# The gate and up products of two feed-forward networks, in a fixed order of slots of one block product

## The chip, the core and the metric

The kernel runs on one core of a Trainium2 chip. It uses five engines, each with a queue of its own that it works through in order: TensorE (PE, with PEld for its weight loads), VectorE (DVE), ScalarE (ACT), GpSimd (POOL), and SyncE (SP), which issues all the DMAs. The metric is the device time of one execution in microseconds; the median of three runs of the kernel before is 2160.37 us (2160.37 to 2164.31).

## The reference

One step of a streaming encoder layer for 1024 + 32 frames of width 1024. It holds two feed-forward networks, one before and one after the token mixer; the change touches these two alone.

```python
def swiglu(h, w_gate, w_up, w_down):
    return (jax.nn.silu(h @ w_gate) * (h @ w_up)) @ w_down

def layer(x, lw, sb_fn, s0, gla_chunk):
    x = x + 0.5 * swiglu(rmsnorm(x, g_ffn1), w1g, w1u, w1d)
    mix, k, v, s = token_mixer(rmsnorm(x, g_mix), ...)
    x = x + mix
    x = x + 0.5 * swiglu(rmsnorm(x, g_ffn2), w2g, w2u, w2d)
    return rmsnorm(x, g_final), k, v, s
```

The inner width is 2816, that is 22 tiles of 128.

## The kernel before, in words

**Numbers in halves.** Every factor of a matmul is stored as a high and a low half: ACT copies the value with rounding into the high half (L94, in `split_to`), DVE subtracts that from the value and leaves the low half (L98). A block product is three matmuls per pair of tiles (high by high, high by low, low by high).

**Gate and up.** A pair of 128-wide tiles of the gate or of the up weights, by all 1056 columns, is one `Step`, computed by Strassen's scheme with seven block products instead of eight. There are 20 steps for each network, even ones for gate and odd ones for up; the first pair is done without Strassen by `Opening`. One block product (`product`, L378) is 24 matmuls of 264 columns. The seven come in the order 1, 6, 7, 5, 2, 4, 3 (`ORDER`); I number their places 0 to 6 and call the time of one product on PE a slot. The seven use four PSUM tiles, `acc_a` to `acc_d`, each of which is one of four buffers: a serves places 0 and 4, b place 1, c places 2 and 5, d places 3 and 6. `after` (L391 to L428) reads a PSUM tile out behind its product: on ACT at place 0 (`s1`, L391), on DVE as `u2` and `u3` at places 1 and 2 (L394, L397), then the four results (L418 or L427 on DVE with a Silu on ACT or a product on POOL; place 4 by ACT or DVE alone). A product that goes on with a PSUM tile waits until it has been read out.

**Beside the products** run three kinds of work:
- the weights of the next step: `load` brings them raw (L330, L331), POOL forms the sums S1 to S4 (L349 to L362), `split_to` makes halves of them (`S1` to `S4`, `A22`, and `whl` for the two unsummed blocks, L98);
- the operands of the down product that follows: `form` (L442) takes differences of finished tiles, `keep` makes halves and stores them (`part_spill`, L451);
- in the first network alone, chores (`Splits`): 52 pieces of the weights that the mixer uses later are loaded (`x<-win`, 256 KB, L77), halved, and stored (`win_split<-x`, 512 KB, L84). They share two buffers in turn, which are parts of the big tile `x`.

**What sets the order.** `gate_up` writes each product down and behind it, at once, all that the product allows: both halves of the next weights, both halves and the store of a finished operand, and a chore's load, halves or store (job n from slot 5n/2 on: load there, halves 3 slots on, store 4 on). The list scheduler of the framework then orders the instructions of each engine by its own estimate of when each is ready. So neither the distance between a first half and a second one, nor the pace of the chores, is fixed by the program: the 52 chores, written over 130 of the 140 slots, ran between 89 and 390 us.

**Down.** `DownStep.prep` forms four sums on POOL and their halves for one Strassen step of the down product; `Down.head` is called at the last gate-and-up step and loads the first operands (`load_part`, L620) and weights (`load_step`, L624). Loads of `x` (L515) into the four tiles that chores and kept operands used stand in `gate_up`'s last step.

Of the kernel before, what the change touches and what calls it, by code (L numbers as in the profile page):

```python
# [54 lines left out]
class Splits:  # L55
# [3 lines left out]
    def __init__(self, S, jobs, bufs):  # L59
        self.S, self.jobs, self.bufs = S, jobs, bufs  # L60
        self.at = {}
        for n in range(2 * len(jobs)):
            slot = 5 * n // 2
            for k, fn in ((0, self.load), (3, self.split), (4, self.store)):
                self.at.setdefault(slot + k, []).append((fn, n))

    def buf(self, n):
        return self.bufs[n % 2][:, :1024]

    def halves(self, n):  # L70
        return self.buf(n).rearrange("p (a n) -> p a n", a=2)

    def cols(self, n):
        return slice(n % 2 * 512, n % 2 * 512 + 512)

    def load(self, n):
        self.S.nc.sync.dma_start(self.buf(n)[:, 512:], self.jobs[n // 2][0][:, self.cols(n)])  # L77

    def split(self, n):
        t = self.halves(n).bitcast(F32R)  # L80
        split_to(self.S, t[:, 0], t[:, 1], self.buf(n)[:, 512:])

    def store(self, n):
        self.S.nc.sync.dma_start(self.jobs[n // 2][1][:, :, self.cols(n)], self.halves(n))  # L84

    def some(self, slot):
        for fn, n in sorted(self.at.pop(slot, ()), key=lambda job: job[1]):
            fn(n)
# [228 lines left out]
class Step:  # L317
# [15 lines left out]
    def split_w(self):  # L333
        w = self.S.wp.tile([P, 2, 1024], F32R, name="whl", tag="w")
        split_to(self.S, w[:, 0], w[:, 1], self.raw0)
        self.W["A11"], self.W["A12"] = w[:, :, :512], w[:, :, 512:]

    def prep(self, p, eng):
# [25 lines left out]
        split_to(S, w[:, 0], w[:, 1], src)  # L364
# [80 lines left out]
    def keep(self, name, src):  # L445

        S = self.S
        S.n_kept = getattr(S, "n_kept", 0) + 1
# [18 lines left out]
def gate_up(S, H, op, steps, among, between, tail, xd, chore):  # L467


    N = len(steps)  # L470
    done = {}

    def prep(t, p):
        if t >= N:
            return
        steps[t].prep(p, S.nc.gpsimd if t else S.nc.vector)
        done[t] = done.get(t, 0) + 1
        if done[t] == 5 and t + 2 < N:
            steps[t + 2].load()

    for j in range(4):
        for n, i in enumerate((0, 1, 2, 3) if j < 3 else (0, 2, 1, 3)):
            op.product(j, i, among(j, n))
            between(j, n)
            if i == 2:
                op.silu()
            if j == 3 and n == 1:
                steps[0].split_w()
                for p in (6, 7, 5):
                    prep(0, p)  # L490
        op.store(j)
        if j == 1:
            steps[0].load()
            steps[1].load()
    for k in range(4):
        H.part("T3", k, 1)
    for p in (4, 3):
        prep(0, p)
    for t in range(N):
        for p in ORDER:  # L500
            steps[t].product(p)
            steps[t].after(p)
            n = ORDER.index(p)
            for back, name in FORMS[t % 2].get(n, ()):
                if t >= back:
                    steps[t - back].form(name)
# [5 lines left out]
            if t == N - 1:  # L512
                if p == 1:
                    for d in range(4):
                        S.nc.sync.dma_start(S.x[d], xd[d])  # L515
                tail(p)
# [10 lines left out]
class DownStep:  # L527
# [6 lines left out]
    def prep(self, raw):  # L534
# [6 lines left out]
        s1, s2, s3, s4 = s12[:, :w], s12[:, w:], s34[:, :w], s34[:, w:]  # L541
        nc.gpsimd.tensor_add(s1, a[3], a[2])
        nc.gpsimd.tensor_sub(s2, s1, a[0])
        nc.gpsimd.tensor_sub(s3, a[0], a[3])
        nc.gpsimd.tensor_sub(s4, a[1], s2)
        tag = ("S1", "A22") if self.odd else ("S2", "S3")
# [5 lines left out]
        split_to(S, wb[:, 0, :w], wb[:, 1, :w], a[2])  # L552
# [43 lines left out]
class Down:  # L596
# [35 lines left out]
    def prep(self, i):  # L632
        if i < len(self.steps):
            self.steps[i].prep(self.raw.pop(i))

    def head(self, p):
# [7 lines left out]
        elif p == 7:  # L644
            self.load_part(0, 4)
            self.load_part(0, 5)
            self.prep(0)
        elif p == 5:
            self.load_part(0, 6)

# [792 lines left out]
def body(tc, A):  # L1443
# [10 lines left out]
    with ExitStack() as top:  # L1454
# [66 lines left out]
        with ExitStack() as es:  # L1521
# [41 lines left out]
            gate_up(S, H, op, steps, among, between, down.head, A["x"], splits.some)  # L1563
# [136 lines left out]
        with ExitStack() as es:  # L1700
# [68 lines left out]
            gate_up(S, H, op, steps, lambda j, n: [], between, down.head, xs, lambda n: None)  # L1769
# [112 lines left out]
```

## Time and profile before

| what | value |
|---|---|
| median of three runs | 2160.37 us |
| the profiled execution's own time | 2163.55 us |
| its span on the core | 2161.8 us |
| PE busy | 2067.5 us (96%) |
| DVE busy | 1454.9 us (67%) |
| ACT busy | 887.7 us (41%) |
| POOL busy | 668.8 us (31%) |
| data moved by DMA | 325.03 MB, 150 GB/s on average |

How to read it: PE is nearly always busy, so the time is PE's own work and the holes in it. An average over the span hides where the holes are; the page's row of PE by 40 slices of 54 us shows 7 tenths in the first slice, then 9, 9, 9, 9, 8, 8 (54 to 378 us), where 9 stands for anything from 90% up, and nines after that. A row of a table of windows gives, for each engine, its busy time and in brackets its number of instructions that began there, then the granted TensorE clock, the share of the DMA engines and what they moved. A row of the waits names who waited for whom, the sum, how often, and the longest wait.

### The profile page before, as it was taken

To read this page: it belongs to the slowest core of one execution; us is meant where nothing else is said; L and a number is where in the kernel's file an instruction comes from. 1 tells how busy PE (TensorE), PEld (TensorE's weight loads), DVE (VectorE), ACT (ScalarE), POOL (GpSimd) and SP (SyncE) were. 2 spreads that over 40 slices of the span, in tenths; PEclk is the share of its full clock that TensorE was granted. 3 is DMA by queue.
4 is the path that set the end of the run, shared out by engine and by line. 5 is a ranking of instruction groups with operands and counts; after the bars stand their busy time and mean duration, and the time that the engine had idled before them with its cause. 6 is when DMAs were issued, how large, how long until landed. Compare 5 with 4: busy or idle time off the path is not lost.

```text
span 2161.8 us, 38696 instructions
## 1 busy us (share of the span) xinstructions
PE 2067.5 (96%) x15636; PEld 1997.3 (92%) x15636; DVE 1454.9 (67%) x2205; ACT 887.7 (41%) x1618; POOL 668.8 (31%) x578
## 2 busy tenths in 40 slices
PE   7999988999999999999999998999999999999997
PEld 6898988999999988888889987899999999999997
DVE  6866677664778556376776677687566666457865
ACT  6543444432223333243654555454333433322333
POOL 0133333444775110011112201101343443458720
PEclk9999999999999999999999999999999999999999
DMA  4277777546854121112133243242334334398322
GB/s 173 81 254 259 262 267 269 204 161 249 339 193 125 69 77 59 63 63 85 37 101 98 78 135 106 85 134 80 120 141 156 142 130 160 129 379 299 108 65 81
DMA packets 128339, 325.03 MB, mean 150 GB/s; under 512 B 12096, under 2 KB 32864, under 8 KB 124832
## 3 DMA queue, kind: packets, MB, share of 16 engines
q1 hardware_dynamic: 128160, 322.56, 42.6%
q8 instruction: 123, 2.02, 0.4%
q14 instruction: 56, 0.46, 0.1%
HBM read 201.72 MB, written 114.03 MB: 146 GB/s over the span
## 4 chain that ended last, share of the span: by engine, by line
PE 69%; DVE 11%; DMA 7%; issue 6%; POOL 4%; ACT 3%; SPq 0%; DVEq 0%; ACTq 0%; POOLq 0%
PE acc_a L378 8%; PE acc_d L378 8%; PE acc_c L378 7%; PE acc L286 4%; PE pj L103 4%; PE acc_b L378 4%; PE pj L105 3%; PE pj L104 3%; PE pd_c L574 3%; PE pd_d L574 3%; PE pd_a L574 3%; PE pd L103 2%; PE pd L105 2%; PE pd L104 2%; DMA win_split<-x 2%
## 5 line engine op out<-in xcount | busy, mean ns | idle before, releaser
L378 PE MATMUL acc_a<-h,whl 128*128 128x264 f32 x1920 | 251.4, 287 | 11.5 <-ACT s L391 9.5
L378 PEld LDWEIGHTS acc_a<-h,whl 128*128 128x128 f32 x1920 | 242.3, 191 | 12.9 <-ACT s L391 10.8
L378 PE MATMUL acc_d<-part,S 128*128 128x264 f32 x1920 | 247.3, 284 | 3.7 <-DVE x L418 3.6
L378 PEld LDWEIGHTS acc_d<-part,S 128*128 128x128 f32 x1920 | 238.7, 188 | 4.7 <-DVE x L418 4.3
L94 ACT ACTIVATE x<-x 128x528 fp32r<-128x528 f32 (+1 forms) x164 | 103.4, 638 | 295.8 <-POOL x L428 81.5
L98 DVE TENSOR_TENSOR x<-x 128x528 fp32r<-128x528 f32 (+1 forms) x164 | 132.1, 814 | 132.7 <-ACT x L94 132.0
L103 PE MATMUL pj<-h,whl 128*128 128x352 f32 x576 | 205.3, 356 | 0.0
L105 PE MATMUL pj<-h,whl 128*128 128x352 f32 x576 | 190.9, 331 | 0.0
L104 PE MATMUL pj<-h,whl 128*128 128x352 f32 x576 | 189.3, 329 | 0.0
L94 ACT ACTIVATE S<-s 128x512 fp32r<-128x512 f32 x160 | 98.2, 623 | 114.7 <-PE acc_d L378 43.1
L428 POOL TENSOR_TENSOR x<-tc,x 128x528 f32<-128x528 f32 x60 | 103.3, 1722 | 123.4 <-DVE tc L427 110.7
L362 POOL TENSOR_TENSOR s<-wraw,s 128x512 f32<-128x512 f32 x38 | 49.8, 1312 | 295.2 <-DVE S L98 295.2
L378 PE MATMUL acc_c<-h,A 128*128 128x264 f32 x960 | 126.7, 288 | 10.1 <-DVE u L397 9.8
L378 PEld LDWEIGHTS acc_c<-h,A 128*128 128x128 f32 x960 | 121.8, 190 | 12.3 <-DVE u L397 12.3
L378 PE MATMUL acc_b<-h,S 128*128 128x264 f32 x960 | 124.7, 285 | 1.5 <-ACT h L94 1.1
L98 DVE TENSOR_TENSOR S<-s,S 128x512 fp32r<-128x512 f32 x160 | 120.8, 756 | 6.3 <-ACT S L94 5.6
L378 PE MATMUL acc_c<-part,S 128*128 128x264 f32 x960 | 123.8, 284 | 1.1 <-DVE hid L298 1.1
L378 PEld LDWEIGHTS acc_b<-h,S 128*128 128x128 f32 x960 | 120.5, 188 | 1.9 <-ACT h L94 1.3
L378 PEld LDWEIGHTS acc_c<-part,S 128*128 128x128 f32 x960 | 119.5, 188 | 1.3 <-DVE hid L298 1.3
L592 POOL TENSOR_TENSOR x<-x,u 128x528 f32<-128x528 f32 x64 | 102.9, 1615 | 49.7 <-DVE x L563 49.4
L103 PEld LDWEIGHTS pj<-h,whl 128*128 128x128 f32 x576 | 110.5, 192 | 5.1 <-issue 1.7
L349 POOL TENSOR_TENSOR s<-wraw 128x512 f32<-128x512 f32 x38 | 51.7, 1360 | 201.4 <-DVE S L98 195.2
(343 smaller groups left out, 4952.3 us busy)
## 6 DMA issues: line engine op xcount, KB each, us to landing
part_spill<-x SPq DMA_DIRECT2D x112, 528.0 KB, 2.8
h<-part_spill SPq DMA_DIRECT2D x64, 528.0 KB, 8.9
part<-part_spill SPq DMA_DIRECT2D x48, 528.0 KB, 9.6
win_split<-x SPq DMA_DIRECT2D x44, 512.0 KB, 4.0
whl<-win_split SPq DMA_DIRECT2D x22, 1024.0 KB, 5.0
wraw<-w1g SPq DMA_DIRECT2D x22, 512.0 KB, 4.8
wraw<-w1u SPq DMA_DIRECT2D x22, 512.0 KB, 4.0
x<-win SPq DMA_DIRECT2D x44, 256.0 KB, 3.6
```

Of the source, the lines that this page charges most:

```text
L94: nc.scalar.activation(hi, src, AF.Copy)
L98: nc.vector.tensor_sub(lo, src, hi.bitcast(F32))
L103: nc.tensor.matmul(out, w[:, 0, wsl], a[:, 0, asl], start=first, stop=False)
L104: nc.tensor.matmul(out, w[:, 0, wsl], a[:, 1, asl], start=False, stop=False)
L105: nc.tensor.matmul(out, w[:, 1, wsl], a[:, 0, asl], start=False, stop=last)
L286: nc.tensor.matmul(out, self.w[i](k, a), quarter(S, k, b, j), start=k == 0 and n == 0, stop=k == KT - 1 and n == 2)
L349: eng.tensor_add(self.s1, a21, a22)
L362: eng.tensor_sub(src, a12, self.s2)
L378: nc.tensor.matmul(t[:, s, :SW], w[:, a, ks], m(k, b, s), start=fresh and k == 0 and n == 0, stop=k == 3 and n == 2, skip_group_check=not ...
L428: nc.gpsimd.tensor_mul(two(hid), t, sg)
L574: nc.tensor.matmul(t[:, s, :SW], w[:, u, k * P : k * P + P], b[:, v, ss(s)], start=fresh and k == 0 and i == 0, stop=k == 1 and i == 2, sk ...
L592: nc.gpsimd.tensor_add(x[r][h], x[r][h], u)
```

## The change

- `Slots` keeps a list of work by slot. `later(k, fn)` puts `fn` k slots on; `split(hi, lo, src, k, then)` puts the high half k slots on, the low half k + 1, and what follows (a store) k + 2. `run` does what stands at the present slot.
- A step's sums are still formed at once on POOL; their high halves come one slot later and their low halves two later (`whl`: in the same slot and the next). A kept operand: high half one slot after it is formed, low half two, store three after.
- A chore that begins at slot k = 5n/2: load at k, high half at k + 2, low half at k + 3, store at k + 4.
- In each slot the read-out of the product stands ahead of the halves, and the halves ahead of the differences and sums.
- The 140 slots are recorded under a manual schedule for all five engines: each engine keeps the order in which the program is written.
- Weights are loaded for the step after next at place 1 of each step. The first down step's sums stay at place 2 (`p == 7`) and its halves move to place 4 (`p == 2`).

```diff
+class Slots:
+    def __init__(self, S):
+        self.S, self.now, self.at = S, 0, {}
+    def later(self, k, fn):
+        self.at.setdefault(self.now + k, []).append(fn)
+    def split(self, hi, lo, src, k, then=None):
+        nc = self.S.nc
+        self.later(k, lambda: nc.scalar.activation(hi, src, AF.Copy))
+        self.later(k + 1, lambda: nc.vector.tensor_sub(lo, src, hi.bitcast(F32)))
+        if then is not None:
+            self.later(k + 2, then)
+    def run(self):
+        for fn in self.at.pop(self.now, ()):
+            fn()
...
 class Splits:
...
+    def plan(self, slots):
+        for n in range(2 * len(self.jobs)):
+            k = 5 * n // 2
...
+            slots.later(k, lambda buf=buf, src=src, cols=cols: dma(buf[:, 512:], src[:, cols]))
+            slots.split(hl[:, 0], hl[:, 1], buf[:, 512:], k + 2, lambda t=t, out=out, cols=cols: dma(out[:, :, cols], t))
...
 class Step:
...
-    def prep(self, p, eng):
+    def prep(self, p, eng, split):
...
-        split_to(S, w[:, 0], w[:, 1], src)
+        split(w[:, 0], w[:, 1], src, 1)
...
     def keep(self, name, src):
...
-        split_to(S, t[:, 0], t[:, 1], src)
-        S.nc.sync.dma_start(S.parts[self.i - 1, PARTS.index(name)], t.bitcast(F32))
+        S.slots.split(t[:, 0], t[:, 1], src, 1, lambda: S.nc.sync.dma_start(out, t.bitcast(F32)))
...
 def gate_up(...):
...
-    for t in range(N):
-        for p in ORDER:
-            steps[t].product(p)
-            steps[t].after(p)
...
-            if p > 2:
-                prep(t + 1, p)
-            if p == 7 and t < N - 1:
-                steps[t + 1].split_w()
-            chore(7 * t + n)
+    steps[2].load()
+    chores(slots)
+    E = mybir.EngineType
+    with S.tc.manual_schedule(engines={E.PE, E.DVE, E.Activation, E.Pool, E.SP}):
+        for t in range(N):
+            for n, p in enumerate(ORDER):
+                steps[t].product(p)
+                steps[t].after(p)
+                slots.run()
+                for back, name in FORMS[t % 2].get(n, ()):
+                    if t >= back:
+                        steps[t - back].form(name)
+                if t < N - 1:
+                    if p > 2:
+                        steps[t + 1].prep(p, S.nc.gpsimd, slots.split)
+                    if p == 7:
+                        steps[t + 1].split_w(slots.split)
+                        slots.run()
+                if n == 1 and t and t + 2 < N:
+                    steps[t + 2].load()
...
+                slots.now += 1
```

What moves is best seen on two engines. First DVE in the first network, in the sixth step (an up step), before: `x_76<-x_76 128x512` is the low half of a chore, `S2` and `S3` are halves of the next step's weights, and `u2`, `u3`, `tc` read out the products of places 1, 2 and 3.

```order
L98 TENSOR_TENSOR S4_2044<-s3_2042,S4_2044 128x512
L98 TENSOR_TENSOR x_76<-x_76 128x512 x2
L394 TENSOR_TENSOR u2_2111<-s1_2077,acc_b_2086 128x528
L98 TENSOR_TENSOR S2_2117<-s2_2115,S2_2117 128x512
L98 TENSOR_TENSOR x_76<-x_76 128x512
L397 TENSOR_TENSOR u3_2146<-u2_2111,acc_c_2121 128x528
L98 TENSOR_TENSOR S3_2154<-s3_2152,S3_2154 128x512
L98 TENSOR_TENSOR x_76<-x_76 128x512
L427 TENSOR_TENSOR tc_2186<-u3_2146,acc_d_2161 128x528
```

The same place after the change; `L448` is a difference for the down product and `128x528` on `x_76` its low half.

```order
L51 TENSOR_TENSOR x_76<-x_76 128x512
L51 TENSOR_TENSOR x_76<-x_76 128x528
L51 TENSOR_TENSOR A22_2011<-wraw2_1636,A22_2011 128x512
L448 TENSOR_TENSOR x_76<-x_76 128x528
L400 TENSOR_TENSOR u2_2104<-s1_2071,acc_b_2079 128x528
L51 TENSOR_TENSOR S4_2045<-s3_2043,S4_2045 128x512
L403 TENSOR_TENSOR u3_2144<-u2_2104,acc_c_2119 128x528
L51 TENSOR_TENSOR x_76<-x_76 128x528
L448 TENSOR_TENSOR x_76<-x_76 128x528
L433 TENSOR_TENSOR tc_2181<-u3_2144,acc_d_2156 128x528
```

Before, four chore halves stand among the read-outs of four slots, one of them directly ahead of `u3`; after, there is one in these slots, and `u2`, `u3` and `tc` have between them only halves whose first half was put one slot earlier.

Second PE at the start of the first network's first step, before: `acc_a` is the product of place 0, `acc_b` of place 1, `acc_c` of place 2; `whl` and `S2` are their weights.

```order
L378 MATMUL acc_b_904<-h0_84,S2_792 128x264 x3
L378 MATMUL acc_b_904<-h1_85,S2_792 128x264 x3
L378 MATMUL acc_b_904<-h2_86,S2_792 128x264 x3
L378 MATMUL acc_b_904<-h3_87,S2_792 128x264 x3
L378 MATMUL acc_c_938<-part0_104,S3_797 128x264
L378 MATMUL acc_a_876<-h0_84,whl_785 128x264
L378 MATMUL acc_a_876<-h1_85,whl_785 128x264 x3
L378 MATMUL acc_a_876<-h2_86,whl_785 128x264 x3
```

The same place after the change.

```order
L384 MATMUL acc_a_878<-h0_84,whl_785 128x264 x3
L384 MATMUL acc_a_878<-h1_85,whl_785 128x264 x3
L384 MATMUL acc_a_878<-h2_86,whl_785 128x264 x3
L384 MATMUL acc_a_878<-h3_87,whl_785 128x264 x3
L384 MATMUL acc_b_906<-h0_84,S2_792 128x264 x3
L384 MATMUL acc_b_906<-h1_85,S2_792 128x264 x3
L384 MATMUL acc_b_906<-h2_86,S2_792 128x264 x3
```

Before, PE did two matmuls of `acc_a`, then the whole of `acc_b` and one matmul of `acc_c`, and then, in the rows shown, went on with `acc_a`; after, it finishes all 24 of `acc_a` ahead of `acc_b`. From the second step on, and in the second network's gate and up, PE's order is the same in both.

More of the change, by code (lines that the diff above doesn't have):

```diff
@@ L464, in gate_up_steps, with gate_up, prep @@
     return steps
-def gate_up(S, H, op, steps, among, between, tail, xd, chore):
+def gate_up(S, H, op, steps, among, between, tail, xd, chores):
     N = len(steps)
[L471 to L479, printed above, removed]
+    slots = S.slots = Slots(S)
+    now = lambda hi, lo, src, k: split_to(S, hi, lo, src)
+    def prep(p):
+        steps[0].prep(p, S.nc.vector, now)
     for j in range(4):
@@ L532, in __init__, with sums @@
         self.odd = m % 2
-    def prep(self, raw):
+    def sums(self, raw):
         S, nc = self.S, self.S.nc
@@ L1562, in body @@
             splits = Splits(S, jobs, (S.x[2], S.x[3]))
-            gate_up(S, H, op, steps, among, between, down.head, A["x"], splits.some)
+            gate_up(S, H, op, steps, among, between, down.head, A["x"], splits.plan)
             nc.vector.tensor_copy(S.identb, consts[:, 0])
@@ L1767, in between @@
                     emit(parts(H))
-            gate_up(S, H, op, steps, lambda j, n: [], between, down.head, xs, lambda n: None)
+            gate_up(S, H, op, steps, lambda j, n: [], between, down.head, xs, lambda slots: None)
             down.strassen(xs)
```

66 lines of the change are left out of this document (28 added, 38 removed).

## The prediction

> **What bounds the kernel now.** I read the table of windows first, by stage, since PE is busy nearly everywhere. The rows are the gate and up of the first network, its three parts, and the gate and up of the second:
>
> ```profile
> 75.50:524.70 449.20, 421.31 (x3365) 416.03 (x3364) 302.45 (x395) 179.35 (x301) 172.79 (x117) 0.99 0.65 229
> 75.50:100.00 24.50, 19.92 (x145) 19.08 (x144) 23.27 (x33) 11.84 (x21) 6.63 (x5) 0.93 0.29 92
> 100.00:400.00 300.00, 276.69 (x2202) 272.29 (x2201) 208.16 (x270) 125.69 (x212) 114.37 (x73) 0.99 0.75 264
> 400.00:524.70 124.70, 124.70 (x1024) 124.66 (x1023) 71.02 (x94) 41.81 (x68) 51.79 (x40) 1.00 0.48 171
> 1480.00:1906.50 426.50, 426.50 (x3500) 426.50 (x3499) 263.40 (x342) 157.90 (x252) 166.61 (x117) 1.00 0.40 146
> ```
>
> The second network has no hole: 3500 matmuls in 426.50 us, 0.1219 us each; a slot of 24 is 2.92 us. From 400 us on the first runs at the same pace (124.70 / 1024 = 0.1218). From 100 to 400 us, while the chores run, 2202 matmuls took 300 us where 2202 x 0.1219 = 268.3 would do: **31.7 us are lost there**, and some more in the first 25 us. No engine is full in these 300 us: DVE has 208, ACT 126. So the loss is waiting. The waits between 75 and 525 us say on whom:
>
> ```profile
> DVE x L98 <- ACT x L94: 92.2, 44, 4.4
> ACT x L94 <- DMA x<-win: 57.0, 24, 5.9
> PEld acc_c L378 <- DVE u L397: 12.3, 10, 2.5
> PEld acc_a L378 <- ACT s L391: 10.8, 6, 2.2
> ```
>
> PE waits for PSUM read-outs (u3, s1), DVE for first halves on ACT, ACT for chores' loads. The timelines of ACT, DVE and PE show one such chain whole (start, length, what, idle time before it):
>
> ```profile
> 208.71 0.63 ACT L94 ACTIVATE x<-x 128x512 fp32r<-128x512 f32 x1 [4.30 <-DMA x<-win]
> 209.37 0.69 DVE L98 TENSOR_TENSOR x<-x 128x512 fp32r<-128x512 f32 x1 [4.04 <-ACT x L94]
> 209.98 0.70 DVE L397 TENSOR_TENSOR u<-u,acc_c 128x528 f32<-128x528 f32 x1
> 210.73 3.21 PE L378 MATMUL acc_c<-h,A 128*128 128x264 f32 x24 [1.51 <-DVE u L397]
> ```
>
> A chore's load is 4.30 us late for ACT, the chore's low half holds DVE 4.04 us, u3 stands behind it, and PE waits 1.51 us for u3. The rows of the chores' loads and stores, by place (count, and the span of time over which they run; the first and the last of them):
>
> ```profile
> L77 SPq DMA_DIRECT2D x<-win x44: 327/333/846, 88.9 to 340.9; - x44
> L84 SPq DMA_DIRECT2D wo_split<-x x8: 519/519/526, 349.1 to 390.2; - x8
> ```
>
> The chores outrun their own buffers: 52 in 89 to 390 us is 5.8 us each, 11.6 us per round of a buffer.
>
> **The opening.** PE's timeline at the first step, and DVE's row of the weights it waits for:
>
> ```profile
> 75.63 0.41 PE L378 MATMUL acc_a<-h,whl 128*128 128x264 f32 x2
> 75.88 1.26 PE L378 MATMUL acc_b<-h,S 128*128 128x264 f32 x9
> 79.01 1.97 PE L378 MATMUL acc_b<-h,S 128*128 128x264 f32 x14 [0.35 <-DVE h L98]
> 83.20 1.22 DVE L98 TENSOR_TENSOR whl<-wraw,whl 128x1024 fp32r<-128x1024 f32 x1
> 84.47 4.47 PE L378 MATMUL acc_a<-h,whl 128*128 128x264 f32 x22 [1.99 <-DVE whl L98]
> 84.50:87.00 2.50, 2.50 (x13) 2.50 (x14) 2.50 (x4) 0.00 (x0) 1.25 (x1) 0.60 0.02 7
> 87.00:90.00 3.00, 3.00 (x22) 3.00 (x20) 3.00 (x6) 0.61 (x1) 0.04 (x1) 0.76 0.29 98
> L378 PE MATMUL acc_d<-part,S x960: 278/283/393, 89.1 to 524.4; 128*128 128x264 f32 x192
> ```
>
> The third matmul of acc_a needs the low half of whl, which DVE ends at 84.4. DVE's order up to there is unchanged, so that moment stays. Before, PE filled the hole with the 24 of acc_b and one of acc_c; now it can't, and does them later: 25 x 0.1219 = 3.0 us. After a hole the granted clock drops: 0.40 x 2.5 + 0.24 x 3.0 = 1.7 us lost in the two window rows. I keep that cost once, as today; with the longer hole (76.0 to 84.4) the clock can be no lower when PE returns than these rows show for a shorter one, unless it falls further, which no row shows.
>
> **The sum.** If nothing waits after 84.47, PE has 140 x 24 - 2 = 3358 matmuls left: 3358 x 0.1219 = 409.3 us, plus 1.7 for the clock, so the last starts at 495.5. Before it starts at 524.4. **Gain 28.9 us.** (The same from the other side: 31.7 lost under the chores and some 0.3 beside them, less the 3.0 of the opening.)
>
> How much is lost could also be read from busy time. The Trainium skill, "Perfetto Trace Analysis", section "Identifying the Most-Contended Engine", says that matmul busy time is a bad measure of headroom because matmuls are pipelined, and wants the share of weight loads or of the work done instead. In the row from 100 to 400 us PE is idle 23.3 us and PEld 27.7, against 31.7 by count: the trace agrees; by matmul idle time the gain would be 8.4 us less.
>
> **Does the new order wait anywhere?** The work of one slot by engine, from the groups between 100 and 400 us:
>
> ```profile
> L98 DVE TENSOR_TENSOR x<-x 128x512 fp32r<-128x512 f32 x51 | 45.0, 881 | 63.3 <-ACT x L94 63.1
> L98 DVE TENSOR_TENSOR S<-s,S 128x512 fp32r<-128x512 f32 x52 | 39.0, 750 | 2.9 <-ACT S L94 2.8
> L98 DVE TENSOR_TENSOR x<-x 128x528 fp32r<-128x528 f32 x44 | 36.4, 826 | 20.3 <-ACT x L94 20.0
> L442 DVE TENSOR_TENSOR x<-x 128x528 f32<-128x528 f32 x24 | 23.4, 975 | 0.3
> L98 DVE TENSOR_TENSOR whl<-wraw,whl 128x1024 fp32r<-128x1024 f32 x14 | 21.3, 1522 | 4.9 <-ACT whl L94 4.9
> L418 DVE TENSOR_TENSOR x<-u,acc_d 128x528 f32<-128x528 f32 x13 | 9.0, 692 | 0.0
> L94 ACT ACTIVATE x<-x 128x512 fp32r<-128x512 f32 x50 | 31.3, 627 | 72.6 <-DMA x<-win 56.8 <-DMA x<-wo 10.7 <-issue 3.0
> L428 POOL TENSOR_TENSOR x<-tc,x 128x528 f32<-128x528 f32 x19 | 33.0, 1738 | 36.8 <-DVE tc L427 36.8
> ```
>
> - *DVE* as a whole: 302 us of work in 411 us, 74%. Its fullest slot is place 3 of a gate step: read-out 0.69, chore 0.88, kept operand 0.83, S2 0.75, whl 1.52, difference 0.98, in all 5.65 us in 2.92. It is 2.7 us late after it; place 4 of a gate step has no DVE read-out and makes up for part. Read-outs come first in a slot, and the nearest use of a PSUM tile after its read-out is two whole slots off (places 2 to 5, 3 to 6, 4 to 0): DVE may be 2 x 2.92 - 0.69 = 5.1 us late before PE waits. Cost 0, with 2.4 us to spare. If the cover goes, every us beyond 5.1 costs PE one in each gate step, ten times in a network.
> - *POOL* now does the three products of an up step before the sum S4 that stood between them; 2 x 1.74 = 3.5 us later for S4, which is needed six slots on. Cost 0.
> - *Halves a slot apart*: the first half is made while DVE works at the slot before, so DVE finds it ready; that replaces the 92 us of DVE behind ACT. What is late next is a chore's load.
> - *The chores*: a buffer's round is five slots, 14.6 us instead of 11.6. From issue to landing (smallest, median, largest), load and store:
>
> ```profile
> DMA to landing us min/median/max: 2.5/3.6/4.8
> DMA to landing us min/median/max: 3.0/4.0/6.7
> ```
>
>  A round is 0.63 + 0.88 + 4.0 + 3.6 = 9.1 us, at the largest landings 13.0, and the order asks for the low half only at 14.6. Cost 0; spare 5.5 us at medians, 1.6 at the worst. SP issues in order, and behind a load that waits for a store stand kept operands' stores and weights' loads; these have a slot or more, the weights six.
> - *Residue*: the first steps, where chores, halves and the late DVE meet for the first time, and slots with the worst landings. One to four stalls like the 1.51 us above, 0 to 6 us; I take 1, nearest to the second network's full row.
> - *The second network* has no chores, and 263 us of DVE in 426: its fullest slot is 4.77 us, 1.9 us late. Cost 0; the same 5.1 us cover it.
>
> **The end of the first network** is the one place with a new competitor. The last operand loads of the down product, their landing, and the DMA window:
>
> ```profile
> 518.93 1.46 SPq L620 DMA_DIRECT2D part<-part_spill  x2
> part<-part_spill SPq DMA_DIRECT2D x1, 528.0 KB, 10.7
> 515.00:520.00 5.00, 5.00 (x43) 5.00 (x43) 2.56 (x4) 1.76 (x3) 1.81 (x1) 1.00 1.04 406
> L515 SPq DMA_DIRECT2D x<-x x4: 328/334/372, 391.3 to 459.9; - x4
> ```
>
> The DMA engines are full at 406 GB/s; the last load lands at about 520.1 + 10.7 = 530.8, and its block begins 6 x 12 matmuls after 524.7, at 533.5: 2.7 us to spare. The four loads of x (4 x 528 KB, 5.3 us at 406 GB/s) ran at 391 to 460; now the chores last to slot 131 of 140 and these loads stand directly ahead of the operands. They start some 3 us before the last step and the operands 1.8 us into it, so 0.5 to 5.3 us are in the way, less the 2.7: 0 to 2.6 us, I take 0.5, since most of it lies in the gap. Halves of the first down step at place 4 rather than 2 are needed at the earliest two slots on, 5.8 us, for four halves of 0.75 us: 0.
>
> 28.9 - 1.0 - 0.5 = 27.4 us. The profiled execution took 2163.55 us over a span of 2161.8; it should become about 2136. The median of the runs is 3.2 us below the profiled one, and I take the difference from that: 2160.4 - 27.4 = **2133 us**.
>
> **Rivals.**
> 1. *The buffers, not the order, are short.* For: 57 us of ACT's waits are for loads into two buffers, and the change adds none. Against: the round needs 9.1 us and gets 14.6. If half of the 31.7 stay: 2133 + 16 = 2149. The Trainium skill, "Perfetto Trace Analysis", section "Optimization Strategy", says that the same gap repeating can mean too little SBUF or PSUM, a count of buffers; by that rule the holes would stay here. The waits quoted come from that limit, but only at the pace of 11.6 us. 8%.
> 2. *Operands late at the end*: the loads of x and the last chores hold the down product's loads for the full 5.3 us, and parts of the 1 MB of its weights (2.6 us) too: 5.3 + 2.6 - 2.7 = 5 us, 2138. 10%.
> 3. *Slower: SP paces PE.* A chore's store and the next load may each wait a slot in SP's queue behind a store whose low half isn't ready. The round is then 9.1 + 2 x 2.92 = 14.9 us, and midway to the largest landings 16.9. In a fixed order PE can't leave the slots behind: 26 rounds x (16.9 - 14.6) = 60 us, 2193. It decides at a round of 14.6, and is slower than before from 14.6 + 27.4 / 26 = 15.7 us. Against: SP's own issues are under 1 us each and stand in the order in which they come ready. 5%.
> 4. *It doesn't do what it says*: the holes come from DMA traffic itself, whoever orders it. Against: from 515 to 520 us the DMA engines are fuller with PE at 5.00 of 5.00. About 2158. 3%.
>
> **How the numbers follow.** My forecast has 74%: 2133, with its own bounds from the residue (0 to 6), the end (0 to 2.6) and the opening (3.0 to 0, if PE fills the hole after all): 2128 to 2140. With rival 2 that is 84%; I leave out rivals 3 and 4 and most of 1, and reach to 2146 for a smaller part of rival 1: 2127 to 2146. About 0.2% (4.3 us) is what a measurement can tell from no change. Faster: 74 + 8 + 10 = 92%; same: 3%; slower: 5%.
>
> **What would show it.** Right: one hole of 8 us at 76 to 84, then PE full to the last gate-and-up matmul at about 496 us; no PE wait for u3 or s1; chores' loads spread to about 460 us; the second network's stage unchanged at 0.1219 us a matmul. Wrong: PE waits for DVE behind place 3; ACT waits on loads that PE's waits follow; PE waits for a load in the first down step; holes in the second network.

## The result, and the profile after

The changed kernel takes 2139.18 us (median of 4 runs, 2136.11 to 2140.95), the kernel before, on the same chip, 2162.34 us (2160.37 to 2165.08): a ratio of 0.9891, with an interval of 0.9871 to 0.9910. It is faster by 23 us; 27.4 were forecast, and the time of 2139 lies in the range of 2127 to 2146. The profiled execution's span went from 2161.8 to 2135.9 us, 25.9 us less; the two profiled executions took 2163.55 and 2137.79 us, so the medians, 23 us apart, hold some scatter of the runs.

The table of windows of the changed kernel, in the columns that the prediction showed:

```profile
75.50:84.50 9.00, 1.73 (x15) 1.52 (x13) 8.79 (x16) 6.22 (x12) 0.00 (x0) 0.79 0.04 14
84.50:87.00 2.50, 1.35 (x6) 1.35 (x7) 2.50 (x4) 0.00 (x0) 0.06 (x1) 0.50 0.16 56
87.00:90.00 3.00, 3.00 (x15) 3.00 (x15) 3.00 (x5) 0.00 (x0) 1.22 (x1) 0.50 0.26 90
90.00:100.00 10.00, 10.00 (x80) 10.00 (x80) 4.74 (x8) 3.46 (x5) 2.58 (x2) 0.95 0.50 159
100.00:400.00 300.00, 300.00 (x2462) 300.00 (x2462) 220.18 (x285) 134.21 (x223) 120.73 (x80) 1.00 0.67 241
```

From 100 to 400 us PE did 2462 matmuls where it did 2202 before. 2462 x 0.1219 is 300.1: nothing is lost there any more. ACT's waits for chores' loads between 75 and 525 us fell from 57.0 us to 12.7, and DVE's waits for chores' first halves from 92.2 to 7.4:

```profile
ACT x L50 <- DMA x<-win: 12.7, 11, 6.1
DVE x L51 <- ACT x L50: 7.4, 8, 1.2
```

The opening, from PE's timeline, and the rows of the last product of a step (first and last start) and of the first down product:

```profile
76.83 0.41 PE L384 MATMUL acc_a<-h,whl 128*128 128x264 f32 x2
85.65 5.21 PE L384 MATMUL acc_a<-h,whl 128*128 128x264 f32 x22 [8.42 <-DVE whl L104]
L384 PE MATMUL acc_d<-part,S x960: 278/283/288, 96.7 to 497.5; 128*128 128x264 f32 x192
L590 PE MATMUL pd_d<-h,whl x288: 278/284/292, 502.0 to 671.1; 128*128 128x264 f32 x144
```

The hole at the opening is there, 8.42 us long, and the last matmul of gate and up starts at 497.5 where it started at 524.4. That is 26.9 us of gain. In the kernel before, the row of the first down product ends at 695.4:

```profile
L574 PE MATMUL pd_d<-h,whl x288: 278/284/425, 528.9 to 695.4; 128*128 128x264 f32 x144
```

695.4 - 671.1 = 24.3, so 2.6 us were given back in the first down product. The second network's first matmul (1497.1 before, 1470.8 after) is 26.3 us earlier again, and the spans differ by 25.9. In gate and up of the second network both kernels take 409.7 us.

### The profile page after: what moved, and what is told of

It reads as the page before. It is cut to its first block, busy times and chain, and to the rows that moved or that the text cites. A ratio compares the mean times of both kernels' runs of the same rounds, so it can differ in the third digit from the quotient of the medians.

```text
span 2135.9 us, 38809 instructions
## 1 busy us (share of the span) xinstructions
PE 2057.9 (96%) x15636; PEld 1991.7 (93%) x15636; DVE 1438.7 (67%) x2205; ACT 885.5 (41%) x1618; POOL 652.8 (31%) x578
## 4 chain that ended last, share of the span: by engine, by line
PE 79%; DVE 9%; issue 4%; DMA 3%; ACT 3%; POOL 3%; SPq 0%; DVEq 0%; POOLq 0%; ACTq 0%
PE acc_a L384 11%; PE acc_c L384 11%; PE acc_d L384 11%; PE acc_b L384 6%; PE acc L292 4%; PE pj L109 4%; PE pj L111 3%; PE pj L110 3%; PE pd_a L590 2%; PE pd_d L590 2%; PE pd_c L590 2%; PE pd L109 2%; PE pd L111 2%; PE pd L110 2%; DMA wraw<-hid_spill 2%
## 5 line engine op out<-in xcount | busy, mean ns | idle before, releaser
L434 POOL TENSOR_TENSOR x<-tc,x 128x528 f32<-128x528 f32 x60 | 100.6, 1677 | 181.2 <-DVE tc L433 139.7
L355 POOL TENSOR_TENSOR s<-wraw 128x512 f32<-128x512 f32 x38 | 58.1, 1530 | 223.2 <-DVE S L104 183.7
L109 PEld LDWEIGHTS pj<-h,whl 128*128 128x128 f32 x576 | 110.2, 191 | 4.8 <-issue 1.5
L50 ACT ACTIVATE S<-s 128x512 fp32r<-128x512 f32 x152 | 93.5, 623 | 46.0 <-PE acc_b L384 18.7
L51 DVE TENSOR_TENSOR S<-s,S 128x512 fp32r<-128x512 f32 x152 | 112.4, 739 | 0.0
L110 PEld LDWEIGHTS pj<-h,whl 128*128 128x128 f32 x576 | 110.4, 192 | 1.0
```

The costliest lines, as they stand in the source:

```text
L50: self.later(k, lambda: nc.scalar.activation(hi, src, AF.Copy))
L51: self.later(k + 1, lambda: nc.vector.tensor_sub(lo, src, hi.bitcast(F32)))
L109: nc.tensor.matmul(out, w[:, 0, wsl], a[:, 0, asl], start=first, stop=False)
L110: nc.tensor.matmul(out, w[:, 0, wsl], a[:, 1, asl], start=False, stop=False)
L355: eng.tensor_add(self.s1, a21, a22)
L434: nc.gpsimd.tensor_mul(two(hid), t, sg)
```

## The experiments

All of them are the changed kernel with an edit, unless the text says otherwise. The table gives the ratio to the kernel before on the same chip, PE's matmuls between 100 and 400 us, what 300 us less 0.1219 us for each of these leaves as lost, and the waits in the same window: ACT's for loads of `x<-win`, and DVE's for first halves in `x` (mostly chores; in f2_pace2_tight and h2_near_same chores alone).

| kernel | ratio (interval) | matmuls | lost, us | ACT for loads, us (longest) | DVE for ACT, us (longest) |
|---|---|---|---|---|---|
| before | 1 | 2202 | 31.7 | 56.8 (5.9) | 83.1 (4.4) |
| changed | 0.9891 (0.9871 to 0.9910) | 2462 | 0 | 11.4 (6.1) | 6.8 (1.2) |
| e1_free_order | 1.0021 (1.0008 to 1.0035) | 2192 | 32.8 | 53.2 (4.7) | 82.9 (4.4) |
| e2_same_slot | 0.9879 (0.9853 to 0.9905) | 2462 | 0 | 8.4 (4.8) | 39.3 (2.8) |
| e4_pace2 | 1.0140 (1.0113 to 1.0168) | 2086 | 45.7 | 131.0 (8.8) | 110.3 (7.1) |
| f2_pace2_tight | 1.0065 (1.0044 to 1.0086) | 2245 | 26.3 | 97.3 (8.2) | 89.1 (6.2) |
| f5_sp_only | 1.0010 (0.9999 to 1.0020) | 2287 | 21.2 | 95.3 (6.7) | 75.8 (5.1) |
| h1_near | 0.9897 (0.9879 to 0.9915) | 2462 | 0 | 40.2 (6.0) | 8.1 (1.2) |
| h2_near_same | 0.9901 (0.9886 to 0.9915) | 2462 | 0 | 58.9 (6.2) | 51.4 (3.5) |
| k1_dve_act | 0.9890 (0.9873 to 0.9906) | 2463 | 0 | 18.0 (3.1) | 6.8 (1.2) |

**The slots without the fixed order.**

```diff
-    with S.tc.manual_schedule(engines={E.PE, E.DVE, E.Activation, E.Pool, E.SP}):
+    if True:
```

> The changed kernel with its distances in slots as written, but without the fixed order: the framework's scheduler orders each engine. Theory (the order on the engines is what counts): the scheduler pulls the chores ahead again, they end near 390 us as before, DVE and ACT wait behind loads, and most of the 31.7 us of holes between 100 and 400 us come back: 2150 to 2160 us. Rival (writing the second half one slot after the first is enough): PE stays full from 90 us on, about 2139 us or, with the opening's hole filled again, 2135 us.

2165.02 us against 2158.95: all of the gain is gone. The window of 300 us reads like that of the kernel before, and so do the waits in the table:

```profile
100.00:400.00 300.00, 276.28 (x2192) 272.42 (x2191) 206.91 (x267) 125.56 (x212) 107.91 (x73) 0.98 0.74 259
```

Writing the halves a slot apart does nothing as long as the scheduler orders them; it puts four chores into a step of seven slots, as in the kernel before, where 2.8 are written. The theory holds. The rest of the change, such as the weights loaded two steps ahead, gains nothing either without the fixed order.

**Both halves in one slot.**

```diff
-        self.later(k + 1, lambda: nc.vector.tensor_sub(lo, src, hi.bitcast(F32)))
+        self.later(k, lambda: nc.vector.tensor_sub(lo, src, hi.bitcast(F32)))
```

> The changed kernel with the low half in the slot of its high half instead of the next one; loads still stand two slots ahead of the high half. Theory (the loss came from loads that were late for a half that stood ahead of a read-out, so the distance from load to halves is what counts): DVE waits 0.6 to 1 us for ACT at most halves, its cushion of 5.1 us covers most of that, PE loses 0 to 6 us: 2139 to 2145. Rival (the distance between the halves is what counts): DVE waits for ACT as it did before, 92 us in this stage, and half or more of the 31.7 us of holes come back: 2155 or more.

2134.7 us, against 2158.95 before, and 2462 matmuls in the 300 us: nothing is lost. DVE waits for ACT 39.3 us there instead of 6.8, and it costs PE nothing.

**The kernel before, with the chores' low halves on POOL.**

```diff
-        split_to(self.S, t[:, 0], t[:, 1], self.buf(n)[:, 512:])
+        split_to(self.S, t[:, 0], t[:, 1], self.buf(n)[:, 512:], pool=True)
```

> The kernel before, in which the low halves of the 52 chores are made by POOL instead of DVE; nothing else is changed. Theory (PE waits since a chore's low half stands on DVE ahead of a read-out): PE's waits for u2, u3 and the results on DVE go, those for s1 on ACT, where the chores' high halves still wait for loads, stay: half of the 31.7 us, about 2145 us. Rival (two buffers are too few, or the DMA traffic itself makes the holes): the chores are as late as before and the holes stay, about 2160 us, or more as POOL's low halves are slower.

2194.77 us, a ratio of 1.0152 (1.0124 to 1.0180), with 1983 matmuls in the 300 us, 58 us lost. The theory's 2145 is far off, and the rival's "about 2160 us, or more" names nothing that would give so much. Two rows of the waits between 100 and 400 us, and ACT's and DVE's timelines at one chore:

```profile
POOL x L96 <- ACT x L94: 86.4, 36, 5.5
DVE S L98 <- ACT S L94: 59.1, 13, 6.6
172.01 0.63 ACT L94 ACTIVATE x<-x 128x512 fp32r<-128x512 f32 x1 [6.13 <-DMA x<-win]
173.20 1.37 DVE L98 TENSOR_TENSOR S<-s,S 128x512 fp32r<-128x512 f32 x1 [4.73 <-ACT S L94]
```

POOL now waits where DVE had waited (86.4 us). But DVE isn't free of the late loads: on ACT the chore's high half waits 6.13 us for its load, the high half of the next weights stands behind it, and DVE waits 4.73 us for that. So the late load reaches DVE by way of ACT's order as well. How much of the 58 us each queue makes isn't shown, and the run doesn't tell the theories apart.

**A chore every two slots.**

```diff
-            k = 5 * n // 2
+            k = 2 * n
```

> The changed kernel with a chore every 2 slots instead of 2.5: a buffer's round is 4 slots, 11.7 us, as long as before the change (11.6), and a load stands right behind the store that it waits for. Theory (order, not pace): the round needs 9.1 us, so PE stays full; from store to high half there are 2 slots, 5.8 us, for landings of 4.0 and 3.6, so ACT waits some 2 us at each chore, which the slot between the halves covers; chores end near 396 us; 2136 to 2141 us. Rival (the slower pace made the gain, the buffers are short at 11.6): holes come back, a third to all of the 31.7 us, 2150 to 2165 us.

2191.78 us: 33 us slower than before in a fixed order, so the theory that the pace doesn't matter fell. SP's, ACT's, DVE's and PE's timelines show a round that doesn't close:

```profile
212.28 0.38 SPq L336 DMA_DIRECT2D wraw<-w1u  x1
212.75 1.13 SPq L337 DMA_DIRECT2D wraw<-w1u  x1
213.94 0.53 SPq L94 DMA_DIRECT2D win_split<-x  x1
222.18 0.33 SPq L93 DMA_DIRECT2D x<-win  x1
225.56 0.63 ACT L50 ACTIVATE x<-x 128x512 fp32r<-128x512 f32 x1 [7.66 <-DMA x<-win]
226.23 0.69 DVE L51 TENSOR_TENSOR x<-x 128x512 fp32r<-128x512 f32 x1 [6.19 <-ACT x L50]
232.00 0.69 DVE L51 TENSOR_TENSOR x<-x 128x512 fp32r<-128x512 f32 x1 [2.50 <-ACT x L50]
235.32 4.71 PE L384 MATMUL acc_c<-h,A 128*128 128x264 f32 x24 [3.51 <-DVE u L403]
```

A chore's store is issued behind two loads of weights (1 MB); the load that reuses its buffer is issued only 8.2 us later, ACT waits 7.66 us, DVE 6.19 and at the next chore 2.50 more, and PE then waits 3.51 us for `u3`. The chores' stores ran from 99.6 to 463.2 us, which is 363.6 / 51 = 7.13 us each and 14.3 a round, not the 11.7 that two slots ask for. Rival 3 of the prediction had the form of it: the landings of store and load, and the two slots that the order puts between high half and store. With the medians of this trace (store 4.9, load 3.1) that is 4.9 + 3.1 + 5.84 = 13.8. Here the order asks for less than this, and PE is slowed to the chores' pace.

**The same pace with a shorter way.**

```diff
-            k = 5 * n // 2
+            k = 2 * n
...
-            slots.split(hl[:, 0], hl[:, 1], buf[:, 512:], k + 2, lambda t=t, out=out, cols=cols: dma(out[:, :, cols], t))
+            slots.later(k + 2, lambda hl=hl, buf=buf: split_to(self.S, hl[:, 0], hl[:, 1], buf[:, 512:]))
+            slots.later(k + 3, lambda t=t, out=out, cols=cols: dma(out[:, :, cols], t))
```

> The changed kernel with a chore every 2 slots as in the kernel e4_pace2, but with the low half in the slot of the high half and the store in the slot after it: one slot instead of two from high half to store, two from store's slot to the high half of the same buffer as there. Theory (a buffer's round in a fixed order is the landings of store and load plus the slots that the order puts between high half and store: in e4_pace2 4.9 + 3.1 + 2 x 2.92 = 13.8 us where 11.7 were allowed): here 4.9 + 3.1 + 2.92 = 10.9 us of 11.7, so few holes, 2136 to 2150 us. Rival (chores every 2 slots are too much traffic or work, however they are ordered): as e4_pace2, 2180 to 2195.

2173.66 us, between the two. The stores ran from 97.6 to 436.2 us, 6.6 us each, 13.3 a round instead of 14.3, and by the ratios 16 us of time came back; the slot that was taken out counts. But the round of 10.9 us from the medians was not kept: stores land late behind the weights again and again (up to 8.9 us), and at this pace nothing makes up for them. The formula with medians gave a direction, not the size.

**The opening.**

```diff
+                if t == 0 and n < 3:
+                    if n == 2:
+                        for q in (6, 7, 1):
+                            steps[0].product(q)
+                        for q in (1, 6, 7):
+                            steps[0].after(q)
```

> The changed kernel in which the first step of each network does the products of places 1 and 2 ahead of that of place 0 on PE, with the read-outs in the old order behind them. Theory (the hole of 8.4 us at the opening is the one place where the fixed order costs): most of it is filled by 48 matmuls, 5.9 us, less what h and hid are late by (2 to 3 us), and the clock falls less behind it: 3 to 6 us faster than the changed kernel, 2133 to 2136. Rival (PE is bound there by the Opening's halves on DVE, and the read-outs that now come together hold up the steps behind them): 0 to 2 us.

2137.56 us, a ratio of 0.9897 (0.9881 to 0.9914): no gain that can be told. PE's timeline:

```profile
80.10 2.72 PE L384 MATMUL acc_b<-h,S 128*128 128x264 f32 x14 [0.35 <-DVE h L104]
88.73 5.43 PE L384 MATMUL acc_c<-part,S 128*128 128x264 f32 x23 [5.69 <-DVE part L104]
```

The product of place 1 fits into the hole, that of place 2 doesn't: its operands `part` are ready only at 88.7, and the wait moved there.

**The fixed order on SP alone.**

```diff
-    with S.tc.manual_schedule(engines={E.PE, E.DVE, E.Activation, E.Pool, E.SP}):
+    with S.tc.manual_schedule(engines={E.SP}):
```

> The changed kernel with the fixed order on SP alone, the queue of all loads and stores; the scheduler orders the other four engines. On DVE it then puts 2.8 chores in a step of seven slots, as in the changed kernel, where it puts 4 with a free SP. Theory (the gain is the pace: the scheduler planned a buffer's round at 3.5 slots, 10.2 us, which the landings and halves don't allow): PE stays full as in the changed kernel, and the opening's hole is filled: 2132 to 2142 us. Rival (the gain is the order of halves and read-outs on DVE and ACT): a third or more of the 31.7 us of holes stays, 2146 to 2160.

2161.62 us, no gain. The stores ran from 96.5 to 495.2 us, 7.8 us a chore, slower than in the changed kernel (101.1 to 471.6, 7.3), and still 21.2 us are lost between 100 and 400. A slow pace alone is not enough. DVE's timeline and PE's at one hole:

```profile
265.61 4.01 DVE L448 TENSOR_TENSOR x<-x 128x528 f32<-128x528 f32 x4 [1.23 <-POOL x L434]
269.54 0.70 DVE L51 TENSOR_TENSOR x<-x 128x528 fp32r<-128x528 f32 x1
270.16 0.70 DVE L400 TENSOR_TENSOR u<-s,acc_b 128x528 f32<-128x528 f32 x1
270.77 0.69 DVE L51 TENSOR_TENSOR S<-s,S 128x512 fp32r<-128x512 f32 x1
271.38 0.68 DVE L51 TENSOR_TENSOR x<-x 128x512 fp32r<-128x512 f32 x1
271.98 0.70 DVE L403 TENSOR_TENSOR u<-u,acc_c 128x528 f32<-128x528 f32 x1
272.73 3.19 PE L384 MATMUL acc_c<-h,A 128*128 128x264 f32 x24 [1.15 <-DVE u L403]
```

In these rows it isn't a late load that holds DVE: it waits 1.23 us for POOL, and then four differences, a kept half, a weights' half and a chore's half stand ahead of `u2` and `u3`; PE waits for `u3`. So work that isn't late can cost PE time too, when it stands ahead of a read-out. This is one hole; over the 300 us chores' loads were late more often than in the kernel before (95.3 us of ACT's waits), and how the 21.2 us divide isn't shown.

**The loads of x a down step later.**

```diff
-        for d in range(4, KT):
-            S.nc.sync.dma_start(S.x[d], xd[d])
...
+                if i == 1 and n < 4:
+                    S.nc.sync.dma_start(S.x[n + 4], xd[n + 4])
```

> The changed kernel in which the four loads of x at the start of each down product stand one down step later, behind the weights of the third step. Theory (in the first down product 2.6 us were lost since these weights came late behind loads of x and operands, at a full DMA): the hole of 2.0 us at 538 us and the slow clock after it go, 1 to 2.6 us, about 2137. Rival (the operands' loads themselves fill the DMA, the order among them doesn't matter): no change within 1 us.

2135.99 us, a ratio of 0.9884 (0.9866 to 0.9902). The last row of the first down product is at 669.0 instead of 671.1:

```profile
L590 PE MATMUL pd_d<-h,whl x288: 278/284/292, 502.0 to 669.0; 128*128 128x264 f32 x144
```

That is 2.1 us earlier, but the reason given isn't seen. In the changed kernel the hole at 538 us looks like this on DVE and PE:

```profile
537.81 1.51 DVE L104 TENSOR_TENSOR whl<-s,whl 128x512 fp32r<-128x512 f32 x2 [1.99 <-ACT whl L100]
539.23 0.70 DVE L579 SCALAR_TENSOR_TENSOR x<-pd_d,x 128x528 f32<-128x528 f32 x1
539.99 1.76 PE L590 MATMUL pd_d<-part,whl 128*128 128x264 f32 x12 [2.01 <-DVE x L579]
```

Low halves that wait for ACT (1.99 us) stand ahead of a read-out of `pd_d`. It is the old trouble of gate and up, in the down product, whose order the scheduler still makes; no wait for the weights is seen at this place. The edit changed the scheduler's order on DVE and POOL there too, and that may be all it did. Nor can the 2.1 us be put down to the edit: from its first `pd_d` row's start to its last, this product takes 169.1 us in the changed kernel and 167.0 here, but also 166.8 in e2_same_slot and 165.9 in h1_near, which leave the loads of x alone. What the edit is worth stays open.

**Halves nearer to their load**, the high half at k + 1, and the low half at k + 2 or, in the second kernel, at k + 1 as well; loads, stores and their order on SP as in the changed kernel.

```diff
-            slots.split(hl[:, 0], hl[:, 1], buf[:, 512:], k + 2, lambda t=t, out=out, cols=cols: dma(out[:, :, cols], t))
+            slots.split(hl[:, 0], hl[:, 1], buf[:, 512:], k + 1)
+            slots.later(k + 4, lambda t=t, out=out, cols=cols: dma(out[:, :, cols], t))
```

> The changed kernel with the chores' halves one slot nearer to their load: load at slot k, high half at k + 1, low half at k + 2; loads and stores stand in the slots of the changed kernel, so the pace, the round of a buffer and SP's order are the same. Theory (what counts is that a load has landed when its half's turn comes on ACT; a load lands 3.1 us or more after its issue, and one slot is 2.92 us): ACT waits 1 to 3 us at most chores, 50 to 100 us in all instead of 12.7, the slot between the halves covers part of it for DVE: 5 to 15 us of PE, 2143 to 2154 us. Rival (the pace is what counts, and the cushion of DVE and ACT covers this): 2136 to 2141 us.

> As h1_near, with the low half of a chore in the slot of its high half (k + 1) too; pace, round and SP's order as in the changed kernel. Theory: DVE now waits at the head of its queue for each late load, as in the kernel before: 10 to 25 us of PE, 2148 to 2163 us, and more than h1_near, where the slot between the halves is insurance. Rival (the pace counts): 2136 to 2142 us, as h1_near.

2136.02 and 2137.7 us: both like the changed kernel, so the theory that the distance from load to half is what counts fell. (The 3.1 us in it are the median landing in the changed kernel; the shortest is 2.6.) The second is the telling one. Its waits between 100 and 400 us, and DVE's and PE's timelines at a late load:

```profile
ACT x L101 <- DMA x<-win: 58.9, 21, 6.2
DVE x L105 <- ACT x L101: 51.4, 29, 3.5
```

```profile
326.86 0.69 DVE L431 TENSOR_TENSOR x<-x,acc_a 128x528 f32<-128x528 f32 x1
331.09 0.69 DVE L105 TENSOR_TENSOR x<-x 128x512 fp32r<-128x512 f32 x1 [3.53 <-ACT x L101]
332.92 0.70 DVE L434 TENSOR_TENSOR tc<-u,acc_c 128x528 f32<-128x528 f32 x1
329.04 3.08 PE L385 MATMUL acc_d<-part,S 128*128 128x264 f32 x24
331.95 3.10 PE L385 MATMUL acc_a<-h,whl 128*128 128x264 f32 x24
```

ACT waits for loads as long as in the kernel before (58.9 us against 56.8), DVE is held for 3.53 us behind one of them, and PE goes from product to product without a gap. What DVE waits for stands behind the read-out of its slot (`L431`), and the next read-out (`L434`) is needed only when PE comes back to that PSUM tile, two slots or more after its product.

**The fixed order on DVE and ACT alone**; PE, POOL and SP are the scheduler's again.

```diff
-    with S.tc.manual_schedule(engines={E.PE, E.DVE, E.Activation, E.Pool, E.SP}):
+    with S.tc.manual_schedule(engines={E.DVE, E.Activation}):
```

> The changed kernel with the fixed order on DVE and ACT alone; the scheduler orders PE, POOL and SP (PE's order stays nearly the same, SP's and POOL's change). Theory (two conditions together: the chores at 2.5 slots, and on DVE and ACT the read-outs of a slot ahead of its halves, so that a late load uses up the cushion of 5.1 us instead of PE's time; SP's order is not the point): PE full from 100 to 400 us, about 2136 us, or 2133 if PE fills the opening's hole. Rival (it is the fixed order of SP against that of the others: in f5_sp_only SP's order and the free engines waited for each other): holes of 5 us or more, 2142 to 2160.

2133.81 us, against 2158.28 before. The window of 300 us is full, and PE fills the opening's hole as it did in the kernel before:

```profile
100.00:400.00 300.00, 300.00 (x2463) 300.00 (x2462) 223.08 (x284) 133.26 (x222) 118.45 (x80) 1.00 0.70 246
L384 PE MATMUL acc_d<-part,S x960: 278/283/291, 89.3 to 492.5; 128*128 128x264 f32 x192
```

The last matmul of gate and up is at 492.5, which is 31.9 us earlier than before, just about the 31.7 that were lost. The chores keep their pace (stores from 96.2 to 467.7 us, 7.3 each). So the order on DVE and ACT, at this pace, is enough for the whole gain in gate and up; the order of PE, POOL and SP needn't be fixed.

**Two repairs together:** the loads of x as in g1_x_later, and place 1 ahead of place 0 on PE in the first step.

```diff
+                if t == 0 and n < 2:
+                    if n == 1:
+                        for q in (6, 1):
+                            steps[0].product(q)
+                        for q in (1, 6):
+                            steps[0].after(q)
```

> The changed kernel with two repairs: the loads of x one down step later as in g1_x_later, and in the first step of each network the product of place 1 alone ahead of that of place 0 on PE (place 2's operands come too late, as f3_opening showed). Theory: 24 matmuls, 2.9 us, go into the hole at 77 to 85 us, the clock falls less behind it, and the first down product gives back 2 us: 2139.2 - 2.9 - 2.1 = 2134, 4 to 6 us below the changed kernel. Rival (what is filled in at the opening waits again behind acc_a's read-out on ACT): only g1's 2 to 3 us, about 2136.

2133.31 us, against 2159.98 before: 0.9876 (0.9861 to 0.9891), the lowest median of all, though k1_dve_act (2133.81) and e2_same_slot (2134.7) are too near to be told from it. PE's timeline at the opening, and the last row of gate and up:

```profile
79.35 1.98 PE L384 MATMUL acc_b<-h,S 128*128 128x264 f32 x14 [0.35 <-DVE h L104]
84.81 4.39 PE L384 MATMUL acc_a<-h,whl 128*128 128x264 f32 x22 [3.24 <-DVE whl L104]
L384 PE MATMUL acc_d<-part,S x960: 278/283/291, 92.0 to 492.8; 128*128 128x264 f32 x192
```

The hole is 3.24 us instead of 8.42, and gate and up ends 4.7 us earlier than in the changed kernel. Of these, 0.85 us were there before the edit could act (its first product begins at 75.98 us instead of 76.83); 2.9 are the 24 matmuls, and 1.0 is the clock, which stays at 0.50 for 3.4 us of PE's work instead of 5.35. The intervals of the two kernels overlap; what shows the gain is the trace.

## Why the prediction was right, and where it was not

**PE full from the opening on: right.** All 31.7 us under the chores came back, and the signs named for "right" came: one hole at the opening, no wait of PE for `u3` or `s1`, the chores' loads spread to 466.7 us. Of the forecast gain of 28.9 us at the end of gate and up, 26.9 were measured. Two terms make the difference.

*The opening began 1.2 us later* (76.83 against 75.63), and so did DVE's weights for it (85.6 against 84.4). This is scatter from run to run, and not the change. PE's first matmul came 0.25 us later, and the matmuls of the stage before, which the change doesn't touch, took their first, longer time until 19.3 us instead of 17. Two matmuls near 17.5 us took 0.61 us before and 1.08 us after:

```profile
17.19 0.61 PE L195 MATMUL st<-sq,ones_d 128*128 128x264 f32 x2
17.81 1.08 PE L201 MATMUL st<-sq,ones_d 128*128 128x264 f32 x2
```

Over all the traces of this case the opening begins between 75.6 and 77.1 us, late where that first stretch is long: 75.68 us in h2_near_same and 77.06 in e1_free_order, where two such matmuls take 0.61 and 1.08 us at that place.

*The clock after the hole cost 2.7 us, where 1.7 were taken:* from 85.65 the 3358 matmuls took 497.5 + 0.1 - 85.65 = 412.0 us instead of 409.3. The prediction said that this clock could be no lower than its rows show, 0.60 and 0.76, "unless it falls further, which no row shows". But these two are means over windows. The clock itself is either 1.00 or 0.50, as rows of narrower windows show, before and after:

```profile
85.00:88.00 3.00, 3.00 (x16) 3.00 (x16) 3.00 (x5) 0.00 (x0) 1.28 (x1) 0.50 0.17 57
85.65:91.00 5.35, 5.35 (x24) 5.35 (x25) 5.35 (x8) 0.10 (x1) 1.27 (x1) 0.50 0.16 54
```

So the clock fell no further; it stayed at 0.50 for longer while PE worked: 3.4 us before (85.0 to 88.4), 5.35 after (85.65 to 91.0). Half of each is the loss, 1.7 and 2.7 us. The term was mis-sized because a mean was read as a level. The residue, taken at 1 us, was 0.

**The end: 0.5 us taken, 2.6 measured** at the end of the first down product, just at the bound of 2.6, but by another mechanism. No wait of PE for the down product's loads is seen; in the one hole of 2.0 us halves stood ahead of a read-out in the down product's own order, and behind it the granted clock was 0.50 from 541.6 to 545.0 us, another 1.7 us. About 2 us were back at the second network's start. By these traces neither can be put down to the change: the first down product takes 165.9 to 170.8 us in the traces of this case (166.5 before, 169.1 after), and from its last row to the second network's first matmul, in stages that no edit touches, eleven traces have 796.9 to 801.7 us (801.7 before, 799.7 after). 26.9 - 2.6 + 2.0 = 26.3, and 25.9 in the span, against 27.4 forecast. That the total came this near is in part luck: these two nearly cancel. The median of 2139.18 us lies at the upper end of the forecast's own bounds of 2128 to 2140.

**The reason: half right.** The prediction put the loss on chores' low halves that stand ahead of read-outs. The timelines show such chains, and e1_free_order and k1_dve_act show that the order on DVE and ACT decides. But it gave the halves a slot apart as what removes DVE's waits, and so PE's. They do remove DVE's waits (92.2 to 7.4 us), and PE needs none of that: in e2_same_slot and h2_near_same DVE waits 39 and 51 us and PE loses nothing. The cushion of 5.1 us, which the prediction worked out for a late DVE, fits this: in the fixed order waits of up to 3.5 us on DVE were covered, and PE lost time where they reached 6.2 and 7.1 us (f2_pace2_tight, e4_pace2). Those two also differ in pace, so the bound itself isn't shown alone. Nor does a run show whether read-outs ahead of halves within a slot, or the due order of slots as a whole, is the part that counts.

**Rival 1 (too few buffers) and rival 3 (SP paces PE)** didn't come at 2.5 slots, but both are near. At 2 slots the same two buffers make the kernel slower than before, much as in rival 3, with a measured round of 14.3 us. The changed kernel's own round by that formula is 3.5 + 3.1 + 5.84 = 12.4 of 14.6 us. The spare of 5.5 us in the prediction left out the two slots in the way of the halves; 2.2 us is nearer. The Trainium skill, "Perfetto Trace Analysis", section "Optimization Strategy", reads a repeating gap as a possible lack of SBUF or PSUM, a matter of the buffer count. Here two buffers give the gap or none by order and pace, so two are enough at 2.5 slots in this order. No run has a third buffer, so whether one would have closed the gaps of the kernel before, or of e4_pace2, isn't shown.

**Rival 4 (the DMA traffic itself)** doesn't explain the holes: from 100 to 400 us k1_dve_act moved 246 GB/s with PE full, while f5_sp_only moved 227 with 21.2 us lost and e4_pace2 217 with 45.7. (The kernel before moved 264, its chores being denser.)

## What to carry to other kernels

When an engine that isn't full holds up one that is, look at what stands directly ahead of the awaited instruction in its queue: the sum of its waits says little (58.9 us of ACT's waits for loads cost nothing in one order, and 56.8 us went with a loss of 31.7 in another). Here a fixed order that puts what the bottleneck needs first and background work behind it turned such waits into slack, and it was enough to fix it on the engines in between. It also ties the bottleneck to the background work, so work out the whole round of a buffer, with the slots in it, before choosing the pace: half a slot less made 23 us of gain into 33 us of loss.

## What the runs showed of the hardware

The granted clock took only two values in these traces, 1.00 and 0.50, so a row's 0.60 or 0.95 says for what part of the window it was halved. Around the hole of 8.42 us in the changed kernel it fell at 80.8 us, some 3.5 us after PE's last matmul, and came back at 91.0, 5.35 us after PE's next: 2.7 us lost. h2_near_same has a hole of 8.42 us as well, but there the clock came back 3.9 us after PE's return (84.51 to 88.4): 2.0 us lost. So the length of the hole alone didn't set the loss.

In the changed kernel a chore's store of 512 KB lands 3.5 us after its issue (median), but one issued right behind 1 MB of weights' loads on the same queue of SP took 8 us. The next load into its buffer waits until the store has landed, so SP's timeline there bounds it:

```profile
237.22 1.08 SPq L337 DMA_DIRECT2D wraw<-w1u  x1
238.75 0.53 SPq L94 DMA_DIRECT2D win_split<-x  x1
246.80 0.33 SPq L93 DMA_DIRECT2D x<-win  x1
```
